# Layer 1's query, key and value projections by Strassen's scheme: seven products of quarters instead of eight

## The chip, the core and the metric

The kernel runs on one core of one Trainium2 chip. The metric is the device time of one execution in microseconds (us), where lower is better. The engines of a core are named as the profile names them: PE (TensorE, matmuls and transposes), PEld (TensorE's weight loads), DVE (VectorE), ACT (ScalarE), POOL (GpSimd) and SP (SyncE, which issues most DMAs).

## The reference, cut to what matters

The program has two layers over 2048 tokens of width 1024. Layer 0 has two attention mixers; the change only puts some extra preparation into it. Layer 1 is differential attention, and its input projection is what is changed:

```python
def odd_layer(x, norm_g, w_in, w_out, qn, kn, ...):
    h = rms_norm(x, norm_g)                       # 2048 x 1024
    proj = h @ w_in                               # w_in: 1024 x 4096
    q, k, v, gate = jnp.split(proj, [1024, 2048, 3072], axis=-1)
    q = rms_norm(q.reshape(b, s, 8, 2, 64), qn)   # per 64 columns
    k = rms_norm(k.reshape(b, s, 8, 2, 64), kn)
    q1, q2 = apply_rope(q[:, :, :, 0], cos, sin), apply_rope(q[:, :, :, 1], cos, sin)
    k1, k2 = apply_rope(k[:, :, :, 0], cos, sin), apply_rope(k[:, :, :, 1], cos, sin)
    ...                                           # attention, gate, w_out, residual
```

Everything is float32. The kernel keeps float32 accuracy with three matmuls for each one: a number is split into a high part H (rounded to the matmul's type, fp32r) and a low part L (what is left), and a product is aH·bH + aH·bL + aL·bH.

## The kernel before, in words

Layer 0's projection runs first (0 to about 560 us), then layer 0's attention with its output projection (to about 1168 us), then layer 1's projection (1168 to 1733 us), then layer 1's attention, gate and output projection.

`_project` serves both layers. The tokens are four blocks of 512, taken in two halves of two blocks. For each half, `hidden` loads a block in four tiles of 128 tokens (line 320), normalizes it (ScalarE squares it, line 323, VectorE scales it, line 325), transposes it on TensorE (line 330) and splits the result into H on ScalarE (line 334) and L on VectorE (line 335). Then groups of 512 weight columns follow; in layer 1 these are values, queries, queries, keys, keys, values. `weights_by` loads a group's 1024 x 512 weights in four DMAs on SP's queue (line 301) and splits them (H on ScalarE, line 307, L on GpSimd, line 309). The L of line 309 reads two tiles in SBUF, as the operations of lines 375, 379 and 381 do. The weights of a group are loaded once per half.

`project_tile` makes one tile of 128 tokens x 512 columns in one bank of PSUM: for each of eight k-tiles, `mm3` issues three matmuls (lines 214 to 216) with 128 x 128 of the hidden tile as the stationary and 512 columns of weights as the moving operand. For queries and keys, `squares` (lines 358, 359) and `normed` follow on the tile: the scaling by the norm reads PSUM (line 369), the rotary part is two products on VectorE (line 375), one on GpSimd (line 379) and a sum (line 381), which in layer 1 alternates between GpSimd and VectorE. `pairs_out` transposes four finished tiles (line 388), splits them and stores them to scratch memory on SP's queue. Values are copied (line 507) and stored from ScalarE's queue.

Two further streams lie in `_project`: `later` splits weights for later stages and stores them, in layer 0 both output projections' weights and in layer 1 the gate's (`AHEAD` says before which groups); and hidden tiles are stored for the gate, which is computed beside layer 1's attention. The last half's first block stays in SBUF for it (`last_hidden`).

Engines execute in order. The framework orders the instructions of each engine by its own estimate of when they become ready, with the order of the source as priority; it can therefore place a transposition between two matmuls of another tile. Buffers come from pools with a fixed count (`bufs`); a pool's next tile waits until the oldest is free. Layer 1's pools lie where layer 0's lay, and the attention's where layer 1's projection lay, so the order in which pools are opened says what must be free before a load can start.

## Time and profile before

| | us |
|---|---|
| median of 3 runs | 2802.15 (2797.86 to 2806.56) |
| the profiled execution: its time | 2806.47 |
| the profiled execution: its span, first to last instruction | 2804.3 |
| TensorE busy in the span | 2691.3 |
| layer 1's projection: first to last matmul | 1168.7 to 1732.7 |

The span is what all views of the trace refer to. The mean granted clock of TensorE is 0.990 of full speed. A matmul's duration in the trace includes its way through the array and overlaps the next one, so a sum of durations isn't the time that TensorE takes; distances between starts are.

### The profile page before, as it was taken

Reading aid. Unit: us, or ns where it says so; the run is one execution under the profiler, and the core shown is the slowest. Engines: PE = TensorE matmul, PEld = TensorE weight load, DVE = VectorE, ACT = ScalarE, POOL = GpSimd, SP = SyncE. Lnnn points to the kernel's source line nnn. Section 1 sums busy time; section 2 is a strip of 40 time slices with the busy share of each in tenths; the row PEclk is TensorE's granted clock in tenths of the full one; section 3 lists DMA queues with packets and bytes.
Section 4 is the critical chain, followed back from the end, with each engine's and each line's share of the span. In section 5 each row is a group of like instructions: output and inputs, shape, how many; then the busy total and the mean of one; then the engine's idle time right before and its main releaser. Section 6 shows DMA issues by size and latency. Waiting matters only on the chain.

```text
span 2804.3 us, 43657 instructions
## 1 busy us (share of the span) xinstructions
PE 2691.3 (96%) x13384; PEld 2166.5 (77%) x13384; DVE 1822.1 (65%) x4520; ACT 1599.4 (57%) x3975; POOL 1431.7 (51%) x1519
## 2 busy tenths in 40 slices
PE   7999999999899999999999999999999999999998
PEld 6888887888788888788888888767676777676776
DVE  7752285336777776457834783478886887777762
ACT  5443544357767775333343332578886777776661
POOL 3641254245545454336453652367675666767671
PEclk9999999999999999999999999999999999999999
DMA  5673348739877774754495347788867676464542
GB/s 177 226 240 139 109 148 271 239 111 248 223 196 192 191 196 144 238 190 128 143 297 187 124 134 211 219 232 225 215 194 223 178 210 200 124 190 134 162 154 80
DMA packets 354041, 521.64 MB, mean 186 GB/s; under 512 B 42768, under 2 KB 137744, under 8 KB 353808
## 3 DMA queue, kind: packets, MB, share of 16 engines
q1 hardware_dynamic: 349200, 510.47, 60.6%
q10 hardware_dynamic: 4608, 8.39, 0.8%
q8 instruction: 107, 1.75, 0.3%
q14 instruction: 126, 1.03, 0.1%
HBM read 361.70 MB, written 157.02 MB: 185 GB/s over the span
## 4 chain that ended last, share of the span: by engine, by line
PE 69%; DMA 7%; DVE 3%; ACT 2%; issue 1%; POOL 1%; SPq 0%; ACTq 0%; DVEq 0%; POOLq 0%
PE cO L1005 8%; PE p1mm L216 6%; PE p1mm L215 6%; PE p1mm L214 6%; PE cS L949 4%; PE cS L950 4%; PE ctr L1001 4%; PE com L214 2%; PE com L215 2%; PE com L216 2%; PE mom L214 2%; PE mom L215 2%; PE mom L216 2%; PE mtrB L775 2%; PE cG L214 2%; PE cG L216 2%
## 5 line engine op out<-in xcount | busy, mean ns | idle before, releaser
L956 ACT ACTIVATE cP<-cS,cnm 128x512 f32<-128x512 f32 (+3 forms) x640 | 394.3, 621 | 145.2 <-DVE cnm L953 134.2
L953 DVE TENSOR_REDUCE cnm<-cS 128x1 f32<-128x512 f32 (+3 forms) x640 | 374.7, 602 | 61.5 <-PE cS L950 55.0
L989 POOL TENSOR_TENSOR cP<-cP,cP 128x512 f32<-128x512 f32 (+1 forms) x320 | 358.3, 1148 | 43.7 <-ACT cP L987 43.1
L988 POOL TENSOR_SCALAR cP<-cP,crl,cel 128x512 f32<-128x512 f32 (+3 forms) x288 | 209.9, 743 | 237.9 <-DVE crl L970 136.1
L214 PE MATMUL p1mm<-p1wH,p1hH 128*128 128x512 f32 x768 | 300.1, 392 | 1.2 <-ACT p1hH L334 1.2
L216 PE MATMUL p1mm<-p1wH,p1hL 128*128 128x512 f32 x768 | 300.4, 392 | 0.0
L215 PE MATMUL p1mm<-p1wL,p1hH 128*128 128x512 f32 x768 | 299.3, 390 | 0.0
L309 POOL TENSOR_TENSOR p0wL<-p0ws,p0wH 128x512 fp32r<-128x512 f32 (+1 forms) x140 | 169.9, 1241 | 247.5 <-ACT p0wH L307 228.4
L1005 PE MATMUL cO<-cpt,cv 128*128 128x512 f32 (+3 forms) x640 | 290.1, 538 | 2.9 <-DVE cpt L1003 2.8
L949 PE MATMUL cS<-ck,cqd 128*128 128x512 f32 (+3 forms) x640 | 265.2, 418 | 17.1 <-ACT cP L956 13.7
L1003 DVE COPY cpt<-ctr 128x512 f32<-128x512 f32 (+1 forms) x320 | 191.4, 605 | 112.5 <-PE ctr L1001 109.1
L214 PE MATMUL p0mm<-p0wH,p0hH 128*128 128x512 f32 (+1 forms) x640 | 237.8, 375 | 6.7 <-ACT p0vt L497 4.7
L216 PE MATMUL p0mm<-p0wH,p0hL 128*128 128x512 f32 (+1 forms) x640 | 238.8, 374 | 1.5 <-DVE p0hL L335 1.5
L950 PE MATMUL cS<-ck,cql 128*128 128x512 f32 (+3 forms) x640 | 233.7, 369 | 5.8 <-DMA cql<-qL 5.8
L215 PE MATMUL p0mm<-p0wL,p0hH 128*128 128x512 f32 (+1 forms) x640 | 238.8, 373 | 0.0
L1001 PEld LDWEIGHTS ctr<-ident,cP 128*128 128x128 f32 x1088 | 139.0, 142 | 120.4 <-issue 64.9
L309 POOL TENSOR_TENSOR p1wL<-p1ws,p1wH 128x512 fp32r<-128x512 f32 x112 | 154.4, 1402 | 137.8 <-ACT p1wH L307 126.6
L987 ACT ACTIVATE cP<-cP,cc 128x512 f32<-128x512 f32 (+1 forms) x320 | 189.1, 651 | 22.9 <-DVE cc L973 22.4
L1001 PE MATMUL ctr<-ident,cP 128*128 128x128 f32 x1088 | 177.1, 275 | 5.2 <-ACT csq L1034 3.6
L214 PEld LDWEIGHTS p1mm<-p1wH,p1hH 128*128 128x128 f32 x768 | 144.3, 188 | 29.9 <-ACT p1hH L334 1.4
L216 PEld LDWEIGHTS p1mm<-p1wH,p1hL 128*128 128x128 f32 x768 | 144.2, 188 | 29.4
L215 PEld LDWEIGHTS p1mm<-p1wL,p1hH 128*128 128x128 f32 x768 | 144.3, 188 | 29.1
(302 smaller groups left out, 6945.4 us busy)
## 6 DMA issues: line engine op xcount, KB each, us to landing
p1ws<-in_od_w_in_dram SPq DMA_DIRECT2D x56, 512.0 KB, 3.7
p0ws<-in_ev_w_in_dram SPq DMA_DIRECT2D x48, 512.0 KB, 4.6
ck<-kH SPq DMA_DIRECT2D x144, 128.0 KB, 3.6
ck<-kL SPq DMA_DIRECT2D x144, 128.0 KB, 3.8
cv<-v SPq DMA_DIRECT2D x72, 256.0 KB, 4.3
cqd<-qH SPq DMA_DIRECT2D x64, 256.0 KB, 5.9
cql<-qL SPq DMA_DIRECT2D x64, 256.0 KB, 7.8
cwH<-wgH SPq DMA_DIRECT2D x64, 256.0 KB, 5.4
```

The source lines that it names most:

```text
L214: mm(ps, aH, bH, start=first, stop=False)
L215: mm(ps, aH, bL, start=False, stop=False)
L216: mm(ps, aL, bH, start=False, stop=last)
L309: low.tensor_tensor(l[:, :width], ws[:, k, :width], f32(h[:, :width]), ALU.subtract)
L949: mm(ps, qd[:, m, js], kt[:, :wd], start=True, stop=False)
L950: self.anchor = mm(ps, ql[:, m, js], kt[:, :wd], start=False, stop=True).ins
L953: nc.vector.tensor_reduce(nm[:, m, z:z + 1], ps, AX.X, ALU.max, negate=True)
L956: exp = nc.scalar.activation(chunks[z][:, :wd], ps, AF.Exp, bias=nm[:, m, z:z + 1], accum_out=acc).ins
L988: nc.gpsimd.tensor_scalar(p1, p1, rl[:, 0:1], e1, ALU.mult, ALU.mult)
L989: nc.gpsimd.tensor_tensor(p1, p1, p2, ALU.add)
L1001: nc.tensor.transpose(turned[:, (j - j0) * P:(j - j0 + 1) * P], us[j][kt // 4][:, kk:kk + P], self.ident)
L1005: mm(O[:, j0 * P:], v, T[:, :wd], start=(kt == 0), stop=(kt == nkt - 1), skip_group_check=True)
```

## The change

`_project` is divided into `project0` (layer 0, as before, but for one new stream) and `project1` (layer 1, new).

**The scheme.** For two blocks of 512 tokens and a group of 512 weight columns, the hidden matrix A (512 tokens x 1024) and the weights B (1024 x 512) are cut into quarters: A's rows into 256 + 256 tokens, the inner dimension into 512 + 512, B's columns into 256 + 256. Instead of eight products of quarters there are seven, by Winograd's form of Strassen's scheme, with four sums of A's quarters (S1 to S4), four sums of B's (T1 to T4) and sums of the products. In `PRODUCTS`, each entry names A's quarter or sum, B's quarter (row, column) or the slot of B's sum, and the bank that accumulates it. Three banks per block (X, Y, Z) accumulate products; X is read several times in between.

**B's sums** are made in layer 0's projection: `weight_sums` has 24 steps, called before each block of a group (26 calls). **A's sums** are made by the new `hidden`, from the transposed quarters while they are in PSUM, and split into H and L (ScalarE and GpSimd). S2 lies in the place of quarter 21, which is only needed by the gate; it is stored and reloaded at the end.

**In each group** a product of a block is 24 matmuls: two token tiles, four k-tiles, three parts, with 256 columns of weights as the moving operand. Results are put together by ScalarE's copies from X and VectorE's additions to them. Norm and rotary part (`normed`) now work on whole quarters, 128 x 1024, and read SBUF.

**Besides:** each weight quarter or sum is loaded and split as one operand of 128 x 1024, one or two ahead; the gate's weights are split one operand at a time, before each query or key group, instead of in two lumps; PSUM is divided into 2 banks for transposes and 6 for products (before 4 and 4); rotary tables are made once per half; halves take blocks (3, 2) and (0, 1); in the attention, pools are opened in another order, and the gate's weights get a pool of their own, `gw`.

```diff
-    AHEAD = ((0, 2), (0, 3), (1, 2), (1, 3)), ((0, 5), (1, 0))
+    AHEAD = (0, 2), (0, 3), (1, 2), (1, 3)
...
+        self.s1["t"] = d("t1", [6, 4, 4, P, 256])
...
                 for bi, b in enumerate(blocks):
+                    if half or gi:
+                        next(sums, None)
...
+    def weight_sums(self, pool):
+        nc, W = self.nc, self.a["od_w_in"]
+        sub = lambda o, x, y, op=ALU.subtract: nc.gpsimd.tensor_tensor(o, x, y, op)
+        for g in range(6):
+            for k in range(4):
+                t = pool.tile([P, 2, 2, 256], F32, tag="ts", name="p0ts")
+                nc.sync.dma_start(
+                    t.rearrange("p r c d -> p r (c d)"),
+                    W[:, g * 512:(g + 1) * 512].rearrange("(r k p) c -> k p r c", r=2, p=P)[k],
+                )
+                b11, b12, b21, b22 = (t[:, r, c, :] for r in range(2) for c in range(2))
+                sub(b22, b22, b12)
+                sub(b12, b12, b11)
+                sub(b11, b22, b11, ALU.add)
+                sub(b21, b21, b11)
+                nc.sync.dma_start(self.s1["t"][g, :, k].rearrange("s p d -> p s d"), t.rearrange("p r c d -> p (r c) d"))
+                yield
+
+    PRODUCTS = (
+        ("11", (0, 0), None, "X"), ("12", (1, 0), None, "Y"), ("s2", None, 0, "X"), ("s3", None, 3, "X"),
+        ("22", None, 2, "X"), ("s1", None, 1, "Z"), ("s4", (1, 1), None, "Z"),
+    )
+    ORDERS = (0, 1, 2, 5, 3, 4, 6), (0, 1, 2, 3, 4, 5, 6)
...
+        st = pool("st", 3)
+        wp = pool("w", 8)
...
+        xp = pool("x", 6)
+        ptr = pool("ptr", 2, space=PSUM)
+        pmm = pool("pmm", 6, space=PSUM)
...
+        def operand(src, *to):
+            ws = st.tile([P, 4, Q], F32, tag="ws", name=n + "ws")
+            nc.sync.dma_start(ws, src)
+            H, L = (wp.tile([P, 4, Q], F32R, tag="w", name=n + "w" + part) for part in "HL")
+            nc.scalar.activation(H, ws, AF.Copy)
+            nc.gpsimd.tensor_tensor(L, ws, f32(H), ALU.subtract)
+            return H, L
...
+                dv = nc.vector.tensor_tensor
+                a21, a22 = turned(1, 0), turned(1, 1)
...
+                nc.scalar.activation(r21, a21, AF.Copy)
+                halves(a22, 4, hi)
+                dv(raws[1], a22, r21, ALU.add)
+                a11 = turned(0, 0)
+                halves(a11, 0, lo)
+                dv(raws[3], a11, r21, ALU.subtract)
+                dv(raws[2], raws[1], a11, ALU.subtract)
+                a12 = turned(0, 1)
+                halves(a12, 4, lo)
+                dv(raws[4], a12, raws[2], ALU.subtract)
...
+                for k in (2, 3, 1, 4):
+                    nc.scalar.activation(of(k, "H"), raws[k], AF.Copy)
+                    nc.gpsimd.tensor_tensor(of(k, "L"), raws[k], f32(of(k, "H")), ALU.subtract)
+                yield
...
+        def normed(C, r, tab):
+            v = C.rearrange("p t (h d) -> p (t h) d", d=HD)
+            sq = tq.tile([P, D], F32, tag="tq", name=n + "sq")
+            nc.scalar.activation(sq, C.rearrange("p t c -> p (t c)"), AF.Square)
+            ss = sm.tile([P, 16], F32, tag="qss", name=n + "qss")
+            nc.vector.tensor_reduce(ss, sq.rearrange("p (h d) -> p h d", d=HD), AX.X, ALU.add)
+            rs = self.rstd(sm, ss, 16, 1.0 / HD, n + "q")
+            nc.vector.tensor_tensor(v, v, rs.unsqueeze(2).to_broadcast([P, 16, HD]), ALU.mult)
...
+            for o in (0, 32):
+                nc.vector.tensor_tensor(
+                    t4[:, :, :, o:o + 32], c4[:, :, :, 32 - o:64 - o],
+                    St[:, 4 * r:4 * r + 4, o:o + 32].unsqueeze(2).to_broadcast([P, 4, 4, 32]), ALU.mult,
+                )
+            nc.gpsimd.tensor_tensor(
+                c4, c4, Ct[:, 4 * r:4 * r + 4, :].unsqueeze(2).to_broadcast([P, 4, 4, HD]), ALU.mult
+            )
+            flat = C.rearrange("p t c -> p (t c)")
+            nc.gpsimd.tensor_tensor(flat, flat, t2, ALU.add)
...
+                    opens = p in (0, 1, 5)
+                    if opens:
+                        ps[bank, bi] = pmm.tile([P, 2, Q], F32, tag="mm", name=n + "mm" + bank)
+                    acc = ps[bank, bi]
+                    for pr in range(2):
+                        for k in range(4):
+                            aH, aL = stationary(h[bi], name, k, pr)
+                            for i, (l, r_) in enumerate(((aH, wH), (aH, wL), (aL, wH))):
+                                mm(
+                                    acc[:, pr, :], l, r_[:, k, :], start=opens and pr == k == i == 0,
+                                    stop=k == 3 and i == 2, skip_group_check=True,
+                                )
+                    two = slice(2 * bi, 2 * bi + 2)
+                    kept = {0: "a", 2: "b", 3: "c", 4: "d"}.get(p)
+                    if kept:
+                        nc.scalar.activation(tile_(kept)[:, two, :], acc, AF.Copy)
+                    if p == 1:
+                        nc.vector.tensor_tensor(T["a"][:, two, :], acc, T["a"][:, two, :], ALU.add)
+                        whole("a", 0, 0, bi)
...
         ld = pool("ld", 2)
-        pp = pool("pp", 20)
+        kp = pool("kp", 4)
+        gw = pool("gw", 3)
+        sm = pool("sm", 8)
+        fin = pool("fin", 2)
         ot = pool("ot", 4)
         vp = pool("v", 4)
+        sb = pool("sb", 2)
+        pp = pool("pp", 20)
```

`whole` calls `normed` on a quarter (two blocks) once both blocks have it, and queues eight turns per query or key group: `turn` transposes four 128 x 128 pieces, splits and stores them, at most one after each product, from the third product on after the quarter was queued. The steps of a query or key group are (product, block) with both blocks of a product in a row; in a value group the second block follows two steps behind the first, which leaves its hidden tiles time.

More of the change, by code (lines that the diff above doesn't have):

```diff
@@ new lines, in tables @@
+            tabs["q"] = self.rope_tables(tb, self.gain["ev_a_q_norm"], -0.125, n + "tq")
+            tabs["k"] = self.rope_tables(tb, self.gain["ev_a_k_norm"], 1.0, n + "tk")
+        groups = [
+            ("qk", 0, 512, dict(tab="q", dH="aqH", dL="aqL", p0=0)),
+            ("akv", 512, 256, dict(tab="k", dH="akH", dL="akL", p0=0)),
+            ("qk", 1280, 512, dict(tab=None, gain=True, dH="bqH", dL="bqL", p0=0)),
+            ("qk", 1792, 512, dict(tab=None, dH="bkH", dL="bkL", p0=0)),
+            ("bv", 2304, 512, {}),
+            ("gate", 768, 512, dict(r0=0)),
+            ("gate", 2816, 512, dict(r0=512)),
+        ]
@@ L338, in hidden @@
                 pass
-            if layer == 1 and b:
-                tok = slice(b * BLK, (b + 1) * BLK)
-                nc.sync.dma_start(s["hH"][:, :, tok].rearrange("k p t -> p k t"), f32(hH))
-                nc.sync.dma_start(s["hL"][:, :, tok].rearrange("k p t -> p k t"), f32(hL))
             return hH, hL
@@ L443, in _project @@
                 h = [hidden(blocks[0], 0)]
-            if layer == 0 and not tabs:
+            if not tabs:
                 tables()
             h.append(hidden(blocks[1], 1))
-            self.last_hidden = h[0]
             for gi, (kind, c0, width, o) in enumerate(groups):
@@ L450, in _project @@
                 ready = None
-                if (half, gi) in self.AHEAD[layer]:
+                if (half, gi) in self.AHEAD:
                     next(ahead)
-                turns = list(enumerate(blocks))
-                if layer == 1 and half == 1 and gi == len(groups) - 1:
-                    turns.reverse()
-                for bi, b in turns:
+                for bi, b in enumerate(blocks):
+                    if half or gi:
+                        next(sums, None)
                     if kind == "gate":
@@ L513, in _project @@
-                if not tabs:
-                    tables()
-            turn()
+                        pairs_out(xs, 4 if kind == "qk" else 1, b, o)
+    def weight_sums(self, pool):
[15 more added lines that the diff above has]
+                yield
```

387 lines of the change are left out of this document (274 added, 113 removed).

## The prediction

> **What bounds the kernel now.** I read the page's busy times first, then the windows by stage, the waits of TensorE in layer 1's projection, that stage's own instructions, and last the timeline for the spacing of matmuls and for what VectorE and GpSimd do to each other.
>
> ```profile
> span 2804.3 us, 43657 instructions
> ...
> PE 2691.3 (96%) x13384; PEld 2166.5 (77%) x13384; DVE 1822.1 (65%) x4520; ACT 1599.4 (57%) x3975; POOL 1431.7 (51%) x1519
> ```
> ```profile
> core 0: us, PE busy (x) PEld busy (x) DVE busy (x) ACT busy (x) POOL busy (x), PEclk, DMA share, GB/s
> 0.00:640.00 640.00, 611.11 (x3063) 513.43 (x3064) 345.57 (x801) 299.21 (x693) 247.71 (x251) 0.99 0.56 185
> 1168.00:1735.00 567.00, 566.19 (x2685) 472.38 (x2686) 354.56 (x598) 199.12 (x408) 259.99 (x194) 1.00 0.55 179
> ```
> ```profile
> PE p1mm L214 <- ACT p1hH L334: 1.2, 1, 1.2
> ```
> The second window is layer 1's projection. TensorE is busy for 566.2 of 567 us at the full clock and waits once, for 1.2 us; GpSimd is busy for 260 us (46%). So this stage is TensorE's alone, and what is taken off TensorE there shortens the run, as long as no other engine takes its place. The stage's matmuls:
>
> ```profile
> L214 PE MATMUL p1mm<-p1wH,p1hH x768: 387/389/477, 1168.7 to 1732.3; 128*128 128x512 f32 x192
> ...
> L216 PE MATMUL p1mm<-p1wH,p1hL x768: 389/389/478, 1169.6 to 1732.7; 128*128 128x512 f32 x192
> ```
> Three lines of 768 make 2304 matmuls of 512 columns in 564 us. The duration in a row (389 ns) overlaps its neighbours; what counts is the distance from start to start:
>
> ```profile
> 1339.96 0.39 PE L214 MATMUL p1mm<-p1wH,p1hH 128*128 128x512 f32 x1
> ...
> 1344.49 0.39 PE L216 MATMUL p1mm<-p1wH,p1hL 128*128 128x512 f32 x1
> 1344.73 1.03 PE L388 MATMUL p1trq<-ident,p1xn 128*128 128x128 f32 x8
> 1345.52 0.48 PE L214 MATMUL p1mm<-p1wH,p1hH 128*128 128x512 f32 x1
> 1345.83 0.40 PE L215 MATMUL p1mm<-p1wL,p1hH 128*128 128x512 f32 x1
> ```
> From 1339.96 to 1344.49 are 20 distances: 0.2265 us each, so 2304 take 521.9 us. Eight transposes push the next matmul 1.03 - 0.23 = 0.80 us back and make its successor 0.08 late: 0.89 per eight. The stage has 368 (256 of queries and keys, 112 of hidden tiles): 40.8 us. Together 562.7 of the 564 measured, so spacing and transposes explain the stage.
>
> **The matmuls.** Each group of 512 columns and each half (two blocks) now runs 7 products x 2 blocks x 2 token tiles x 4 k x 3 parts = 336 matmuls, against 192 before, but of 256 columns. Over 6 groups and 2 halves: 4032. Before shows that size in layer 0's narrow key and value group, with the same operands:
>
> ```profile
> 83.74 0.28 PE L215 MATMUL p0mm<-p0wL,p0hH 128*128 128x256 f32 x1
> ...
> 88.54 0.28 PE L216 MATMUL p0mm<-p0wH,p0hL 128*128 128x256 f32 x1
> ```
> ```profile
> 84.83 0.19 PEld L216 LDWEIGHTS p0mm<-p0wH,p0hL 128*128 128x128 f32 x1
> 84.94 0.19 PEld L214 LDWEIGHTS p0mm<-p0wH,p0hH 128*128 128x128 f32 x1
> ```
> 40 distances in 4.80 us: 0.120 us. A weight load (0.19 us) starts every 0.12 as well, so it stays covered at this width. Halving the width costs 0.120 x 2 against 0.2265, 6% more per column, and eats half of the eighth that the scheme saves: 4032 x 0.120 = 483.8, **-38.1 us** (not the 65 that 7/8 of 521.9 would give). The Trainium skill (TensorE: Matmul & The Clock Gate, Back-to-back issue gap) gives N/2.4 + 2.5 ns for a full clock: 109 and 216 ns. By it the saving would be an estimated 57 us and the time some 19 us lower; the rows here are 11 ns above it at both widths, and the measurement decides.
>
> **Transposes.** The number is the same. They now come from two banks of PSUM instead of four, so they may run in fours, each with its own late successor: 46 more times 0.085 = 4 at most, 0 at least. I take +2.
>
> **Query and key groups: GpSimd and VectorE.** This is where the change adds most. Each weight operand is now loaded and split per half (84 operands of 1024 columns, and 8 for the gate, against 112 of 512), and GpSimd does both multiply and add of every rotary quarter.
>
> ```profile
> L309 POOL TENSOR_TENSOR p0wL<-p0ws,p0wH 128x512 fp32r<-128x512 f32 x124 | 157.7, 1300 | 235.6 <-ACT p0wH L307 216.4 <-DMA wo1L<-p0wL 9.9 <-ACT p0sq L358 9.0
> L309 POOL TENSOR_TENSOR p1wL<-p1ws,p1wH 128x512 fp32r<-128x512 f32 x112 | 154.4, 1402 | 137.8 <-ACT p1wH L307 126.6 <-DMA wgH<-p1wH 7.8 <-DMA kH<-p1eH 2.6
> ...
> L309 POOL TENSOR_TENSOR p0wL<-p0ws,p0wH 128x256 fp32r<-128x256 f32 x16 | 12.4, 788 | 12.0 <-ACT p0wH L307 12.0
> ```
> From 256 to 512 columns an operation grows by 512 ns, so 1024 take 1300 + 1024 = 2.32 us; twice the stage's mean, 2.80, is the upper end. A query or key group of a half has 8 operands and 4 quarters of two operations: 16 x 2.32 = 37.1 us. VectorE adds to that, since the two shut each other out:
>
> ```profile
> L381 DVE TENSOR_TENSOR p1xn<-p1xn,p1t x32: 1751/1762/1771, 1237.5 to 1695.5; 128x512 f32<-128x512 f32 x32
> ```
> ```profile
> L369 DVE TENSOR_TENSOR p1xn<-p1mm,p1q8r x64: 680/686/693, 1232.4 to 1691.0; 128x512 f32<-128x512 f32 x64
> ```
> ```profile
> L375 DVE TENSOR_TENSOR p1t<-p1xn,p1tqS x64: 412/419/1522, 1233.6 to 1600.6; 128x256 f32<-128x256 f32 x64
> ```
> ```profile
> L325 DVE SCALAR_TENSOR_TENSOR p1xt<-p1xt,p1xr,p1g_in x16: 1280/1285/2408, 1133.5 to 1482.2; 128x1024 f32<-128x1024 f32 x16
> ```
> ```profile
> 1237.47 1.28 POOL L381 TENSOR_TENSOR p1xn<-p1xn,p1t 128x512 f32<-128x512 f32 x1
> ```
> ```profile
> 1237.54 1.76 DVE L381 TENSOR_TENSOR p1xn<-p1xn,p1t 128x512 f32<-128x512 f32 x1 [0.81 <-POOL p1xn L379]
> ```
> With one input in PSUM (L369) a 512 wide operation takes 686 ns, never more. With both in SBUF (L381) it takes 1762, and the pair in the timeline shows why: GpSimd ends at 1238.75, VectorE at 1239.30, 0.55 later; it stood still until GpSimd was done. The Trainium skill (GPSIMD Engine Reference, Key points) says the same: the two share SBUF interfaces, with contention from VectorE instructions that have two SBUF inputs. The two rows speak against this change, because the scaling by the norm, until now from PSUM, will read a tile in SBUF. Per quarter VectorE needs 1.285 (1024 wide, L325) and two 512 wide at about 0.70 (between L375's 0.42 and L325): 2.68, four times 10.7, less 0.13 of each of the 12 that runs under GpSimd's end: 9.1. The shared way is thus taken for 46.2 us, against TensorE's 336 x 0.120 + 32 x 0.111 = 43.9. The group took until now:
>
> ```profile
> 1250.66 0.87 PE p1trq L388 x8
> ...
> 1392.01 0.87 PE p1trq L388 x8
> ```
> Three groups in 141.35: 47.1 us. TensorE's part sinks by 3.2, but the shared way lets it sink by 0.9 only. The transposes of a finished quarter wait for GpSimd's addition, and behind them on TensorE's queue stand the next products. If nothing absorbed it, 2.3 us in each of 8 groups is 18; the value groups, where GpSimd has 7 x 2.32 = 16 us of work beside 40 of TensorE, and the operands fetched ahead absorb some. Bounds 0 and, with 2.80 per operand and 2.6 per rotary operation, (43.2 + 10.7 - 43.9) x 8 = 80. Taken, nearest to 46.2 with half absorbed: **+9**.
>
> **Hidden tiles at the start and between the halves.** The sums of the hidden quarters are made here.
>
> ```profile
> L334 ACT ACTIVATE p1hH<-p1trh 128x512 fp32r<-128x512 f32 x29 | 16.0, 594 | 12.4 <-PE p1trh L330 10.0 <-DMA wgL<-p1wL 2.3
> ...
> L323 ACT ACTIVATE p1junk<-p1xt 128x1024 f32<-128x1024 f32 x13 | 13.8, 1058 | 13.8 <-DMA p1xt<-x 13.8
> ```
> A block cost ScalarE 4 x (1.06 + 2 x 0.59) = 9 us; now it is twice 2 x 1.06 + 9 x 0.6 = 15. Between the last use of the first block's old tiles and the first need of the second block's new ones lie 8 steps of 24 matmuls, 23 us, against 30 for the two blocks, of which the 8 of squares can run ahead. It just fits on paper; but the loaded rows, the raw sums and the products' results share six buffers, so each half block's load waits for the one before. Two places, 0 to 8 each: **+6**. Bank X is copied (0.59) between products 3 and 4, with only one step between them, in value groups at times none: +1 (0 to 5).
>
> **Layer 0.** 24 steps each load 512 KB, do four 256 wide operations on GpSimd (4 x 0.79 = 3.2 us) and store 512 KB.
>
> ```profile
> POOL p0wL L309 <- ACT p0wH L307: 200.7, 33, 35.1
> ...
> ACT p0wH L307 <- DMA p0ws<-in_ev_w_in_dram: 43.0, 20, 7.6
> ```
> ```profile
> SPq L301 <- POOL p0wL L309: 105.1, 44, 6.7
> ```
> GpSimd waits there for 200 us with nothing to do, which covers 24 x 3.2 = 76. SyncE's queue is the risk: each store waits for GpSimd, and behind it stand the weight loads (L301), for which ScalarE waits already. 0 if that stays covered, 24 x 3.2 = 76 if each step came bare; nearly all is covered: **+3**. Moved besides: the gate's weights leave two places for one eighth per query or key group (counted above); tables are loaded twice, off the path. The hand-over to the attention has a hole of its own:
>
> ```profile
> 1750.00:1760.00 10.00, 3.64 (x10) 2.36 (x10) 3.50 (x8) 4.77 (x12) 1.69 (x3) 0.62 0.51 155
> ```
> 6.4 us idle; the second block's tiles now come free only two steps before the end, and the first key and query loads go into their place. Between -6 and +6; 0 taken, as the gate's matmuls can fill it.
>
> **Sum:** -38.1 + 2 + 9 + 6 + 1 + 3 = -17. The profiled run took 2806.47 (span 2804.3), 4.3 above the median of 2802.15, so 2789; against the median 0.6% faster. What a measurement here can tell from no change is about 0.3%, 8.4 us: 2793.7 to 2810.6 counts as the same.
>
> **Rivals.** First, *the shared way sets the pace* (slower). Every GpSimd operation at the stage's contended duration, and a queue in order that idles while VectorE is shut out: a group of 50 us costs (50 - 43.9) x 8 = 49, so -38 + 49 + 12 = +23: 2829, from 2811 up to 2860 at 53.9. It decides from a group period of 47.2 on, where -38 + 12 is used up; I stand at 45, close by. For it: 46.2 of bare work, 1762 against 686. Against it: GpSimd is at 46% now, and over the whole stage its work (92 + 64 operations of 2.32 and 40 of 1.29) is 414 us, with VectorE's share some 500 of 527. Second, *given back at the seams*: hidden tiles 16, layer 0 8, bank 4, the rest as above, -38 + 2 + 9 + 28 = +1, or less: 2800 to 2808, no change. Six buffers for three uses speak for it, TensorE's one wait of 1.2 us at these places now against it. Third, *everything absorbed*: -38 + 2 + 3: 2773; the average over the stage speaks for it, four query and key groups in a row against.
>
> **Chances.** Forecast (2778 to 2796) 0.46, absorbed 0.16, seams 0.15, shared way 0.23. Faster: 0.16 and 0.42 of the 0.46; same: 0.04, the seams' 0.12 and 0.02 of the shared way; slower: the rest. The range goes from 2768 (absorbed, with a gain at the hand-over) to 2826, the nearer half of the first rival.
>
> **What would show it.** 4032 matmuls of 256 columns at 0.120 us; a query or key group's period of about 45 (at 50 the first rival holds); GpSimd near 85% busy in the stage, and VectorE's 1024 wide scaling well over 1.285 on average; TensorE's waits in the stage some 15 to 20 us, most of them transposes for GpSimd's addition. It would be wrong if 256 wide matmuls ran further apart, or if TensorE waited for weights that GpSimd still splits.

## The result and the profile after

The changed kernel takes 2922.34 us (median of 4 runs, 2917.79 to 2927.30), the kernel before in the same runs 2800.01: a ratio of 1.044 (95% interval 1.041 to 1.047). It is slower by 122 us, where 2789 was forecast. The profiled execution has a span of 2916.0 us, 111.7 more than before.

That execution was the fastest of the four. The page's first lines and its row of granted clock, then two windows: layer 0's first part and layer 1's projection (columns as in the prediction).

```profile
span 2916.0 us, 47395 instructions
...
PE 2696.0 (92%) x15112; PEld 2248.2 (77%) x15112; DVE 1933.4 (66%) x4436; ACT 1680.0 (58%) x4011; POOL 1651.3 (57%) x1603
...
PEclk9999999999999999799998999999999999999999
```
```profile
0.00:640.00 640.00, 600.72 (x2993) 502.57 (x2994) 359.13 (x768) 291.19 (x667) 317.62 (x336) 0.99 0.67 220
1177.00:1836.00 659.00, 560.05 (x4380) 549.59 (x4380) 441.26 (x513) 280.92 (x454) 418.64 (x191) 0.91 0.57 180
```

The projection went from 564 us to 663 (1176.9 to 1839.8), with TensorE idle for 99 of the 659 in the row and at 0.91 of its clock; before it was idle for less than one, at 1.00. In layer 0's window TensorE is busy for 600.7 us, against 611.1 before. What it waits for in layer 1's projection (each row: total us, how often, the longest):

```profile
PE p1trq L656 <- DVE p1eL L659: 45.0, 7, 10.1
PE p1trh L562 <- DVE p1xt L556: 38.6, 6, 11.6
...
PE p1mmX L759 <- ACT p1hH L567: 6.1, 8, 1.0
PE p1trq L656 <- POOL p1cd L649: 3.6, 5, 1.0
PE p1mmX L759 <- ACT p1cc L766: 2.5, 1, 2.5
PE p1trq L656 <- POOL p1cb L649: 1.4, 1, 1.4
```

Two waits carry it: the transposes of finished quarters (`p1trq`), whose two banks come free only when VectorE has made the low parts, and the transposes of x (`p1trh`), which wait for VectorE's scaling. The spacing of the matmuls is as forecast; from the timeline:

```profile
1199.77 0.28 PE L759 MATMUL p1mmX<-p1wH,p1hH 128*128 128x256 f32 x1
...
1202.17 0.28 PE L759 MATMUL p1mmX<-p1wH,p1hL 128*128 128x256 f32 x1
1214.09 2.89 PE L562 MATMUL p1trh<-ident,p1xt 128*128 128x128 f32 x12 [11.64 <-DVE p1xt L556]
...
1218.05 0.41 PE L759 MATMUL p1mmX<-p1wL,p1hH 128*128 128x256 f32 x1
...
1221.67 0.41 PE L759 MATMUL p1mmZ<-p1wL,p1s1H 128*128 128x256 f32 x1
```

20 distances in 2.40 us are 0.120. Behind the wait of 11.64 us the same matmuls run 0.213 apart (17 distances in 3.62 us), and the granted clock is half of full speed until they are back at 0.120:

```profile
1214.09:1222.10 8.01, 7.32 (x33) 6.69 (x34) 3.08 (x5) 5.24 (x9) 4.35 (x4) 0.50 0.59 193
```

The stage has 13 waits of 2.5 us and more; in the 4 us behind them the granted clock was 0.50 to 0.74. So each of these waits is paid a second time in clock.

VectorE's operations in the stage, and the one group of GpSimd that grew most:

```profile
L208 DVE TENSOR_TENSOR p1qu<-p1qu,p1qms 128x16 f32<-128x16 f32 x32 | 50.4, 1575 | 1.1
...
L633 DVE TENSOR_REDUCE p1qss<-p1sq 128x16 f32<-128x1024 f32 x32 | 38.8, 1213 | 13.3 <-ACT p1sq L631 13.3
L206 DVE TENSOR_SCALAR p1qms<-p1qss 128x16 f32<-128x16 f32 x32 | 30.5, 953 | 0.8
L207 DVE SCALAR_TENSOR_TENSOR p1qu<-p1qy 128x16 f32<-128x16 f32 x32 | 26.8, 836 | 1.8 <-ACT p1qy L205 1.7
L635 DVE TENSOR_TENSOR p1cb<-p1cb,p1qr 128x1024 f32<-128x1024 f32 x8 | 21.6, 2706 | 0.2
L209 DVE SCALAR_TENSOR_TENSOR p1qr<-p1qu,p1qy 128x16 f32<-128x16 f32 x32 | 18.5, 579 | 1.1
```
```profile
L517 POOL TENSOR_TENSOR p1wL<-p1ws,p1wH 128x1024 fp32r<-128x1024 f32 x92 | 227.4, 2476 | 104.2 <-ACT p1wH L516 94.6
```

An operation on 128 x 16 elements should be nothing; L208 takes 1.58 us on average. The timeline shows why (VectorE, then GpSimd):

```profile
1347.18 0.17 DVE L209 SCALAR_TENSOR_TENSOR p1qr<-p1qu,p1qy 128x16 f32<-128x16 f32 x1
...
1355.19 1.84 DVE L207 SCALAR_TENSOR_TENSOR p1qu<-p1qy 128x16 f32<-128x16 f32 x1
1357.07 2.34 DVE L208 TENSOR_TENSOR p1qu<-p1qu,p1qms 128x16 f32<-128x16 f32 x1
1359.44 0.18 DVE L209 SCALAR_TENSOR_TENSOR p1qr<-p1qu,p1qy 128x16 f32<-128x16 f32 x1
```
```profile
1354.60 2.40 POOL L649 TENSOR_TENSOR p1cc<-p1cc,p1t 128x1024 f32<-128x1024 f32 x1
1356.96 2.42 POOL L517 TENSOR_TENSOR p1wL<-p1ws,p1wH 128x1024 fp32r<-128x1024 f32 x1
```

L207 ends at 1357.03 with GpSimd's L649 (1357.00), L208 at 1359.41 with L517 (1359.38). With GpSimd idle they take 0.17, as L209 at 1347.18. The four tiny operations thus cost 126 us in place of some 22.

As a measure of the query and key groups I use three whole groups of a half (the second query group and both key groups), from the first copy out of bank X of the second query group to that of the last value group. TensorE alone needs 3 x 43.9 = 131.7 for them by the prediction's rows.

### The profile page after: what moved, and what is told of

It is laid out like the page before. It is cut to its first block, busy times and chain, and to the rows that moved or that the text cites. A ratio compares the mean times of both kernels' runs of the same rounds, so it can differ in the third digit from the quotient of the medians.

```text
span 2916.0 us, 47395 instructions
## 1 busy us (share of the span) xinstructions
PE 2696.0 (92%) x15112; PEld 2248.2 (77%) x15112; DVE 1933.4 (66%) x4436; ACT 1680.0 (58%) x4011; POOL 1651.3 (57%) x1603
## 5 line engine op out<-in xcount | busy, mean ns | idle before, releaser
L517 POOL TENSOR_TENSOR p1wL<-p1ws,p1wH 128x1024 fp32r<-128x1024 f32 x92 | 227.4, 2476 | 104.2 <-ACT p1wH L516 94.6
L759 PE MATMUL p1mmX<-p1wH,p1hH 128*128 128x256 f32 x576 | 168.1, 292 | 8.6 <-ACT p1hH L567 6.1
L516 ACT ACTIVATE p1wH<-p1ws 128x1024 fp32r<-128x1024 f32 x92 | 96.4, 1056 | 125.8 <-PE p1mmX L759 48.7
L759 PE MATMUL p1mmX<-p1wH,p1hL 128*128 128x256 f32 x576 | 166.2, 289 | 0.0
L759 PE MATMUL p1mmX<-p1wL,p1hH 128*128 128x256 f32 x576 | 166.2, 289 | 0.0
L1240 PEld LDWEIGHTS cS<-ck,cqd 128*128 128x128 f32 x640 | 122.1, 191 | 46.3 <-ACT cP L1247 16.3
L215 PEld LDWEIGHTS p0mm<-p0wH,p0hH 128*128 128x128 f32 x640 | 121.3, 190 | 31.0 <-ACT p0vt L447 9.5
```

Source lines behind the costliest of these rows:

```text
L215: mm(ps, aH, bH, start=first, stop=False)
L517: nc.gpsimd.tensor_tensor(L, ws, f32(H), ALU.subtract)
L759: mm(acc[:, pr, :], l, r_[:, k, :], start=opens and pr == k == i == 0, stop=k == 3 and i == 2, skip_group_check=True,)
L1240: mm(ps, qd[:, m, js], kt[:, :wd], start=True, stop=False)
```

## The experiments

The theories are named in the expectations: P (VectorE stands still behind GpSimd's running operation), W (only the sum of the work counts), S (the making of the operands at the two seams, which are the start of layer 1's projection and the change from its first half to its second), later B (bursts: VectorE is behind only where several quarters finish close together). All rows below: median, ratio to the kernel before with its interval, three groups in half 1 / half 2, and TensorE's waits for the scaling of x, with those that the profile puts down to its root. All times are in us.

| run | us | ratio | three groups | x waits |
|---|---|---|---|---|
| the change | 2922 | 1.044 (1.041 to 1.047) | 159.9 / 155.8 | 38.6 |
| e1 half operations | 2906 | 1.036 (1.030 to 1.042) | 150.1 / 149.4 | 38.7 |
| e2 no refinement | 2910 | 1.037 (1.032 to 1.043) | 151.5 / 145.6 | 39.4 |
| e3 low parts on VectorE | 2902 | 1.035 (1.028 to 1.042) | 146.3 / 145.2 | 39.2 |
| e4 x buffers | 2949 | 1.051 (1.043 to 1.059) | 160.4 / 155.8 | 53.8 |
| e5 before + sums | 2814 | 1.003 (1.002 to 1.005) | | |
| e6 before + pools | 2809 | 1.002 (1.000 to 1.004) | | |
| e7 loads first | 2911 | 1.038 (1.036 to 1.040) | 160.0 / 156.0 | 19.4 |
| e8 transposes later | 2934 | 1.046 (1.044 to 1.049) | 160.3 / 155.9 | 39.8 |
| f1 no head norm | 2863 | 1.019 (1.015 to 1.024) | 131.3 / 131.3 | 40.2 |
| f2 no norms, loads first | 2828 | 1.008 (1.006 to 1.010) | 131.3 / 131.3 | 8.6 |
| f3 = e2 + e3 + e7 | 2881 | 1.026 (1.022 to 1.029) | 146.0 / 145.8 | 19.7 |
| f4 pipelined halves | 2899 | 1.034 (1.032 to 1.036) | 160.6 / 155.8 | 6.2 |
| f5 = f4 + e2 + e3 | 2873 | 1.024 (1.022 to 1.026) | 144.8 / 145.4 | 6.1 |
| f6 = f4 + f1 | 2836 | 1.011 (1.009 to 1.013) | 131.3 / 131.3 | 13.0 |
| f7 = f5 + e8 | 2873 | 1.024 (1.021 to 1.027) | 146.3 / 142.4 | 4.5 |
| f8 = f5, rotary on VectorE | 2848 | 1.016 (1.013 to 1.019) | 130.1 / 131.3 | 10.4 |
| f9 = f4 + f10 | 2860 | 1.020 (1.018 to 1.023) | 136.1 / 133.6 | 11.7 |
| f10 GpSimd's work on VectorE | 2880 | 1.028 (1.025 to 1.031) | 136.1 / 133.6 | 42.6 |

The ratios' intervals of e1 to e4 and of e8 overlap the change's. What is read from these five rests on their groups and waits; their medians alone prove nothing.

**e1: GpSimd's operations in halves.**

```diff
-            nc.gpsimd.tensor_tensor(L, ws, f32(H), ALU.subtract)
+            for c in (0, 2):
+                nc.gpsimd.tensor_tensor(L[:, c:c + 2, :], ws[:, c:c + 2, :], f32(H[:, c:c + 2, :]), ALU.subtract)
```
(and the rotary's multiply and add likewise)

> The change's kernel, with the three 1024-element GpSimd operations of layer 1's projection (the operand's low part, the rotary's multiply and its add) cut into two of 512 elements each: the same work, in pieces of half the length. Theory P (VectorE's small operations of the norm, and its operations with two operands in SBUF, stand still until the GpSimd operation that is running ends; in the changed kernel the four tiny ones of the norm take 126 us instead of some 22, and the wait delays the low parts that the transposes' banks wait for): the tiny ones' mean falls to about half, a query or key group from 55 us to 50 to 52, the kernel by 20 to 40 us, to 2880 to 2900. Theory W (only the sum of GpSimd's and VectorE's work counts, however it is cut): the same 2922, or up to 10 us more for the added starts. Theory S (the loss is in the value groups and the making of the operands): the same time, groups at 55 us whatever the tiny ones do.

The four tiny operations went from 3.94 us a quarter (1575 + 953 + 836 + 579 ns) to 3.32, not to half. The longest single one fell from 2.39 to 1.35 us, with the length of GpSimd's pieces, but the second piece follows the first at once and more of them meet one: L209's mean rose from 579 to 986 ns. Still the wait for the low parts fell from 45.0 to 16.0 us (the line of the waits below) and a group by 3 us, though GpSimd's work grew. That is P's sign, against W; but the kernel's 16 us is less than P said.

```profile
PE p1trq L659 <- DVE p1eL L662: 16.0, 12, 5.0
```

**e2: the root without refinement.**

```diff
-            rs = self.rstd(sm, ss, 16, 1.0 / HD, n + "q")
+            ln, rs = (sm.tile([P, 16], F32, tag="q" + t, name=n + "q" + t) for t in ("ln", "r"))
+            nc.scalar.activation(ln, ss, AF.Ln, bias=self.eps, scale=1.0 / HD)
+            nc.scalar.activation(rs, ln, AF.Exp, scale=-0.5)
```

> The change's kernel, with the head norm's reciprocal root taken from ScalarE's Ln and Exp alone: the refinement by four tiny VectorE operations (128x16) is left out, so the roots are a little less exact. Theory P: these four are 126 us of VectorE's time in the stage, nearly all of it standing still behind GpSimd; without them the query and key groups go from 55 us to 49 to 51 and the kernel falls by 30 to 50 us, to 2870 to 2890; part of the standstill moves to the next operation with two operands in SBUF, the norm's multiply. Theory W: the four are worth their free time only, 32 groups of four at 0.17 us, 22 us spread over 8 groups, so a group falls by at most 2.7 us and the kernel by 0 to 20 us. Theory S: the same 2922.

The groups fell from 52.6 to 49.5 us, as P said, the kernel by 12 only, where P had 30 to 50 and W 0 to 20; so this run doesn't part the two. The standstill moved on to the next operations with two inputs in SBUF: the rotary products on b with the key table (L643 there) went from 1.08 to 2.68 us on average.

**e3: the low parts on VectorE.**

```diff
-            nc.gpsimd.tensor_tensor(L, ws, f32(H), ALU.subtract)
+            nc.vector.tensor_tensor(L, ws, f32(H), ALU.subtract)
```

> The change's kernel, with the weights' low parts in layer 1's projection (84 subtractions of 1024 elements, and 8 for the gate weights) on VectorE in place of GpSimd. It takes 227 us off GpSimd and puts 92 operations of about 1.2 us, some 110 us, on VectorE, which works 540 to 550 of the stage's 659 us now, standstills included. Theory P: far fewer standstills, since GpSimd then works about 190 us of the stage; query and key groups 46 to 48 us, the kernel 50 to 75 us faster, 2850 to 2870. Theory W (the sum of the two engines' work is what limits a group): the sum falls from about 46 to 40 us a group, so the groups go to 44 to 47 us and the kernel falls by about as much; what tells it from P is the run with the halved operations. Theory S: the groups may fall but the value groups stay at some 58 us each and the waits of the operands' transposes at 38 us, so that at least 40 us of the loss stays. If VectorE is the limit by its own count, nothing falls: 2910 to 2940.

L208 fell from 1575 to 241 ns:

```profile
L208 DVE TENSOR_TENSOR p1qu<-p1qu,p1qms 128x16 f32<-128x16 f32 x32 | 7.7, 241 | 0.9
```
Groups of 48.6 us and -20 us: the direction of P, but short of 46 to 48, and P and W aren't parted. The waits for x stayed, as S said.

**e4: eight buffers for x, six for the weights.**

```diff
-        wp = pool("w", 8)
+        wp = pool("w", 6)
...
-        xp = pool("x", 6)
+        xp = pool("x", 8)
```

> The change's kernel, with eight buffers in place of six in the pool that the inputs' tiles, the raw sums and the results' quarters share, and six in place of eight for the weights' operands. Theory S (the operands are made late at the two seams since the loads of x wait for one of six shared buffers): the waits of the transposes of x for their scaling fall from 38.6 us to 15 to 25 and the kernel by 15 to 30 us, to 2890 to 2907. Theory P: the query and key groups stay at 55 us and the kernel within 10 us of 2922; fewer weight operands can cost up to 10 us. A variant of S in which the chain load, square, scaling, transposes is what is long, and not the buffer: the waits stay at 30 to 40 us.

The median is 26 us higher, and the waits for x rose to 53.8. The two sizes changed together and moved the pools behind them, so this says nothing on the shared buffers by itself.

**e5 and e6: the kernel before, with the sums alone and with the pools alone.** e5 adds `weight_sums`, its scratch tensor and its pool to the kernel before; e6 opens the attention's pools as the changed kernel does:

```diff
+        kp = pool("kp", 4)
+        gw = pool("gw", 3)
+        sm = pool("sm", 8)
+        fin = pool("fin", 2)
...
-        place = {(h, NB - 1): (ld, ("wH", "wL")) if h < 3 else (kp, ("k0", "k1")) for h in (0, 1, 2, 6, 7)}
+        place = {(h, NB - 1): (gw, ("wH", "wL")) if h < 3 else (kp, ("k0", "k1")) for h in (0, 1, 2, 6, 7)}
```

> The kernel before, with the weights' sums made in layer 0 as in the changed kernel (96 GpSimd operations, their loads and stores, two buffers more) and used by nobody: layer 1's projection stays as it was. It prices layer 0's part alone. In the two traces layer 1's projection starts 8.2 us later in the changed kernel (1176.9 against 1168.7 us). If the sums are what costs that: 8 us, 2805 to 2812 us. If it is the first operands of layer 1, which wait for something else: 0 to 4 us, 2800 to 2805.

> The kernel before, with only the changed kernel's new order of the attention's pools and its own pool for three gates' weights. It prices the hand-over's part alone: from the end of the projection to the end the changed kernel takes 1076 to 1080 us, the kernel before 1069 to 1072. If the new order is the cause: 6 to 11 us more than before, 2806 to 2812. If the cause is that the first queries and keys leave the projection late: the same within 4 us.

The sums cost 9 us (5 to 13), the pools 5 (0 to 11); the medians are 2 us above and inside the expected ranges.

**e7: a block's four loads first.**

```diff
+            loaded = {}
+            for p in range(2):
+                for e in range(2):
+                    t = b * NTB + 2 * e + p
+                    loaded[p, e] = xp.tile([P, D], F32, tag="x", name=n + "xt")
+                    nc.sync.dma_start(loaded[p, e], x[t * P:(t + 1) * P, :])
```

> The changed kernel, with the four loads of x for one block's operands issued ahead of that block's two halves in place of two and two. Theory S1 (a half's operands are late since its loads are only issued when the half before is nearly done, and take 5 to 6 us to land): the chain of a half, 16 us long, gets some 6 us shorter for every second half; waits of the transposes of x 38.6 to 20 us, kernel 15 to 30 us faster, 2890 to 2907. Theory S2 (the chain is ScalarE's squares, VectorE's root and scaling, and the transposes' own evictions, and a load that lands early only waits): the waits stay above 33 us and the time within 8 us. Four loads at once also take four of the six shared buffers, and the first sums get the last two: if these are short, 5 to 10 us slower.

The waits for the scaling fell by 19 us as S1 said (12.2, and 7.2 now put down to the root), and 4.7 of it came back as waits for the raw sums (5.1, before 0.4); the kernel gained 11, where S1 had 15 to 30.

**e8: transposes six products behind.**

```diff
-                                later.append((count[0] + 3, (T[up], T[low], bj, b, hp, o, o["p0"] + 2 * c + hp)))
+                                later.append((count[0] + 6, (T[up], T[low], bj, b, hp, o, o["p0"] + 2 * c + hp)))
```

> The changed kernel, with the transposes of finished quarters put six products behind them in place of three (one number). Theory B (bursts): a group's four quarters don't finish evenly; three of the four norms come within 14 us, each some 8 us of VectorE's queue with its standstills, so VectorE is some 10 us behind when the first transposes need their low parts, although over a whole group its work fits. Then three products more, 8.6 us, let VectorE catch up: the wait of the transposes for the low parts falls from 45 us to under 15, query and key groups from 54 to 47 to 50 us, the kernel by 25 to 50 us, to 2870 to 2900. Theory W (VectorE and GpSimd are short over the whole group): the wait only moves to a later place (the quarters' buffers, the shared banks), groups stay at 52 to 54 us and the kernel within 8 us of 2922.

Nothing moved in the groups; the kernel's median is 12 us higher. Theory B fell here, and again in f7.

**f1 and f2: the norms left out.** f1 returns at the head of `normed`; f2 also drops the squares and the root of x, on top of e7's loads:

```diff
-                    nc.vector.scalar_tensor_tensor(xs[e], xs[e], r[:, e:e + 1], gain, ALU.mult, ALU.mult)
+                    nc.vector.scalar_tensor_tensor(xs[e], xs[e], 0.02, gain, ALU.mult, ALU.mult)
```

> The changed kernel with the norm and the rotary embedding of the queries and keys left out altogether: the quarters go to the transposes as the products leave them. It leaves out 10 VectorE, 3 ScalarE and 2 GpSimd operations for each of 32 quarters. Theory P and theory W both: the query and key groups are held by this work, so they fall from 54 us to TensorE's own 44 to 45 and the kernel by 75 to 85 us, to 2835 to 2850; the value groups and the waits for the scaling of x stay (38 us of waits). If the groups were held by the quarters' way through the shared banks, their buffers or the 256-wide products themselves, they would stay above 48 us and the kernel above 2865.

> The kernel of the run without the head norm, in which also the norm of x is left out (its squares and its reciprocal root; a constant stands in their place, the scaling stays) and a block's four loads of x are issued first. If the seams are the serial way load, squares, root, scaling, transposes: the waits of x's transposes fall from 38 us to 10 to 18, and the kernel by another 25 to 45 us against the run without the head norm, to 2795 to 2820. If the scaling and the transposes' evictions are what is slow: 0 to 15 us. With both left out, what remains over the forecast's 2773 for everything absorbed is layer 0's and the hand-over's part, some 20 us, and the seams' rest.

The three groups of f1, and its whole stage, in the windows' columns:

```profile
1318.49:1449.83 131.34, 131.34 (x1106) 131.34 (x1105) 29.04 (x42) 50.63 (x73) 57.52 (x25) 1.00 0.72 217
1185.11:1782.01 596.90, 548.35 (x4404) 541.00 (x4404) 159.48 (x257) 234.75 (x358) 260.81 (x127) 0.94 0.66 200
```

TensorE is busy for all 131.34 us: 43.8 a group. So the groups' loss is the head norm's, 59 us of time; I had put 75 to 85 on it. (It leaves out eight VectorE operations a quarter, not ten: 513 in the change's stage, 257 in f1's.) f1's stage still takes 596.9 us against 526.6 for TensorE alone (483.8 + 40.8 + 2 by the prediction), and waits 40.2 us for x; with the norm of x out and the loads early, another 36 us go. So S has its own share. f2 came out 8 us above its range.

**f3 to f6: do the edits add up, and is the seam a question of order?** Here a half is one of the two pairs of 128-token tiles from which a block's operands are made. On top of e7's loads, f4 issues such a half's squares, root and scaling ahead of the transposes of the half before it, and begins one product earlier at the change of the projection's halves:

```diff
+            ready_ = {0: scaled(0)}
+            yield
+            for p in range(2):
+                if p == 0:
+                    ready_[1] = scaled(1)
+                xs = ready_[p]
```

> The changed kernel with three of the edits tried before together: the weights' low parts on VectorE, the head norm's root from ScalarE alone (the refinement left out), the loads of x first. One by one they gave 20, 12 and 11 us. Theory P (VectorE's standstills behind GpSimd): the first edit already took most of the standstill, so the second gives only its remaining 64 us of VectorE's time, and together the groups come to 47 to 48 us, the kernel to 2870 to 2885. Theory W (VectorE's queue as a whole): each edit adds its part in full, 43 us, to 2879 or less. In no case does it come under the kernel before: the seams still cost some 50 us, layer 0 and the hand-over some 15 to 20.

> The changed kernel with the making of the operands pipelined by one half: loads of x first, and the squares, the root and the scaling of a half issued before the transposes of the half ahead of it, the first ones one product earlier at the mid seam. All work is kept. Theory S1 (issue order: each half's chain only starts when the half before has been transposed, so 16 us a half lie bare): the waits for the scaling fall from 38 us to 5 to 15 and the kernel by 25 to 45 us, to 2877 to 2897; of that the early loads alone gave 11. Theory S2 (what a half costs is its transposes, four sums and eight evictions on ScalarE and VectorE, 12 us whatever comes first): within 8 us of the run with the loads first, 2903 to 2919.

> The run before this one with also the weights' low parts on VectorE and the head norm's root from ScalarE alone (the refinement left out). If the causes add: f4's time less 30 to 35 us (these two edits with the loads first gave 2881 where the loads alone gave 2911), 2845 to 2870. If they share the same cover: less than 20 us below f4. In no case under the kernel before by the sums so far: 2803 plus layer 0 9, pools 5, and what is left of the head norm, about 30.

> The pipelined making of the operands with the head norm and the rotary left out: the seams alone. Without the pipelining that was 2863, and with the norm of x left out and the loads first 2828. Theory S1: 2825 to 2840. Theory S2: 2848 to 2863. TensorE alone would give 2773 and with layer 0's and the pools' 14 us 2787; what stays above it is the seams' own way, transposes, sums, evictions and the slow clock behind each wait.

f4's wait for the scaling:

```profile
PE p1trh L575 <- DVE p1xt L561: 6.2, 2, 4.0
```
It fell from 38.6 us, with all work kept, and the kernel by 23; without the head norm the same edit gives 27 (2863 to 2836). So the waits for the scaling were a question of when the work is issued (S1), the kernel's gain just short of its range; the seams as a whole were that only in part, since f6's stage still takes 569.2 us against 526.6. In the groups the edits did not add: e3 alone gave 48.6, e2 and e3 together 48.6 again. f3's kernel nevertheless gained 41 of the 43 us that W's sum asks for, inside P's range too, and f5 came out 26 us under f4, between its two theories; neither run parts P and W. In f5's timeline the standstill has moved to what stands next beside GpSimd's rotary, the norm's multiply:

```profile
1302.98 3.43 DVE L650 TENSOR_TENSOR p1cb<-p1cb,p1qr 128x1024 f32<-128x1024 f32 x1
...
1314.95 1.21 DVE L650 TENSOR_TENSOR p1ca<-p1ca,p1qr 128x1024 f32<-128x1024 f32 x1
```

**f7 and f8: what holds the groups at 48.5.** f7 has e8's edit. f8:

```diff
-            nc.gpsimd.tensor_tensor(
+            nc.vector.tensor_tensor(
                 c4, c4, Ct[:, 4 * r:4 * r + 4, :].unsqueeze(2).to_broadcast([P, 4, 4, HD]), ALU.mult
             )
             flat = C.rearrange("p t c -> p (t c)")
-            nc.gpsimd.tensor_tensor(flat, flat, t2, ALU.add)
+            nc.vector.tensor_tensor(flat, flat, t2, ALU.add)
```

> The run with all the edits (2873 us), with the transposes of finished quarters put six products behind them in place of three. Theory B (bursts: VectorE is full for some 30 us of a group and then idle for some 10): with the standstills mostly gone the room of 8.6 us more is enough, the waits for the low parts fall from 23 us to under 10, three groups from 145 us to 135 to 140, the kernel by 12 to 28 us, to 2845 to 2861. Theory W (VectorE short over the whole group, 82% to 85% busy and the rest in places where it cannot be used): within 6 us of 2873; up to 10 us slower if the quarters' six buffers come free too late.

> The run with all the edits, with the rotary's multiply and add on VectorE too, so that GpSimd does nothing in the query and key groups. Theory P (the standstills are what is left: in that run the norm's multiply still takes up to 3.4 us in place of 1.2 and the low parts 2.8 in place of 1.2, some 18 us of 145 over three groups): VectorE loses these 18 us and gets 24 operations of 1.2 us, 29 us: about the same busy time, 45 us a group, in one queue without waits for the other engine: three groups 138 to 146 us, the kernel within 12 us of 2873. Theory W: VectorE's work per group goes from 34 us without standstills to 44, as much as TensorE's own 43.8; three groups 150 to 165 us and the kernel 10 to 45 us slower.

f7 changed nothing. f8 gave the busier engine more work, and the three groups went to TensorE's own time, 130 and 131 us; W had 150 to 165, and even P had only 138 to 146.

**f9 and f10: the engine move with all the computation kept.** f10 is the change with e3's and f8's diff and nothing else; f9 has f4's order too.

> The run with the pipelined making of the operands (2899 us), with the weights' low parts and the rotary's multiply and add on VectorE in place of GpSimd; all the computation kept. Theory P (two engines that stand still for each other): VectorE now does the whole of the norm in one queue, 34 us a group without standstills plus 10 for the rotary and 3 for the refinement, 46 to 47; three groups 131 to 142 us, the kernel 2848 to 2865. Theory W: VectorE's 47 us a group is over TensorE's 43.8, three groups 142 to 150, 2865 to 2885.

> The changed kernel with only this one edit: the weights' low parts and the rotary's multiply and add on VectorE in place of GpSimd. Nothing is left out and the order of the operands' making is the changed kernel's. Theory P: three groups from 160 and 156 us to 131 to 142; the standstills gone, the kernel 40 to 58 us faster, 2864 to 2882; the waits for the scaling of x stay at 38 to 40 us. Theory W: VectorE has more work than before, three groups 142 to 155; 2885 to 2915. Nothing near 2803 in either case, since the value groups' waits stay.

The change, then f10: three groups of each half, and f10's tiny operations.

```profile
1304.79:1464.66 159.87, 137.86 (x1107) 137.05 (x1105) 141.13 (x146) 67.71 (x108) 117.23 (x49) 0.93 0.57 178
1639.59:1795.43 155.84, 137.54 (x1107) 136.25 (x1105) 135.78 (x139) 67.75 (x108) 116.34 (x49) 0.95 0.57 183
```
```profile
1315.44:1451.56 136.12, 135.38 (x1138) 135.14 (x1136) 124.80 (x187) 65.27 (x104) 0.00 (x0) 1.00 0.63 200
1622.58:1756.15 133.57, 132.85 (x1117) 132.61 (x1115) 122.24 (x180) 65.58 (x105) 0.00 (x0) 1.00 0.65 206
```
```profile
L208 DVE TENSOR_TENSOR p1qu<-p1qu,p1qms 128x16 f32<-128x16 f32 x32 | 5.5, 171 | 0.2
...
L206 DVE TENSOR_SCALAR p1qms<-p1qss 128x16 f32<-128x16 f32 x32 | 5.4, 170 | 0.1
```

GpSimd is idle in these windows, where it was busy for 117 us. VectorE has 41 operations more, and its own busy time fell from 141 to 125 us, since the standstills went. TensorE is busy for 135.38 of 136.12 us at a clock of 1.00: f10's windows are longer than f1's 131.34 since another order of instructions puts more of TensorE's work into them (1138 and 1117 instructions against 1106), not since it waits.

The wait for the low parts is at 6.0 us, and the kernel gained 42 us by this edit alone; the waits for x, forecast at 38 to 40, are 42.6, so S's part is untouched. f9 adds the two edits: 2860. No version comes under the kernel before.

The edit takes away two things at once, the standstills and GpSimd's slower pace. That the pace matters little is argued from waits: TensorE waited 5.0 us for GpSimd's additions in the change and 45.0 for VectorE's low parts, and the later transposes of e8 changed nothing; no run parts the two.

## Why the prediction was wrong, by its own steps

In spans, 111.7 us more: the stage starts 8.2 later, takes 98.5 longer (564.4 to 662.9) and leaves 5.0 more behind it (1071.2 to 1076.2). The stage, from its first to its last matmul:

```profile
1176.93:1839.81 662.88, 563.25 (x4404) 552.59 (x4404) 441.95 (x513) 280.92 (x454) 418.64 (x191) 0.92 0.57 180
```

- **Matmuls, -38.1, and transposes, +2: right.** 0.120 us apart; f1's group takes 43.8 against 43.9 worked out. TensorE's own need fell from 564.4 to 526.6.
- **Query and key groups, +9 (0 to 80): the step that failed first.** It set 46.2 us for the way that GpSimd and VectorE share, by three VectorE operations a quarter (2.68 us), and took 45 for a group. A group took 52.6, and the head norm cost 59 us of the kernel's time: 66 of the stage (662.9 against f1's 596.9, which f1's trace enters 8.2 later), 51 of them idle and 15 in slow matmuls. The four tiny operations of the root were not in the list: they have almost no work of their own, but shut out they took 3.94 us a quarter, more than the three counted. The trace before already showed them standing still, at 1.42 us together (two tiles) where four times 0.17 is 0.68:

```profile
L206 DVE SCALAR_TENSOR_TENSOR p1q8u<-p1q8y 128x16 f32<-128x16 f32 x32 | 16.9, 528 | 6.5 <-ACT p1q8y L204 6.3
L207 DVE TENSOR_TENSOR p1q8u<-p1q8u,p1q8ms 128x16 f32<-128x16 f32 x32 | 12.8, 399 | 0.8
L205 DVE TENSOR_SCALAR p1q8ms<-p1qss 128x16 f32<-128x16 f32 x32 | 9.3, 292 | 1.1
L208 DVE SCALAR_TENSOR_TENSOR p1q8r<-p1q8u,p1q8y 128x16 f32<-128x16 f32 x32 | 6.6, 206 | 0.8
```
  And the price doesn't fall on a sum: it falls on VectorE's queue, 47 us busy in a group (141.13 / 3). Behind it in order stand the low parts, behind these two banks, and behind the banks TensorE. The first rival named that ("a queue in order that idles while VectorE is shut out") and its 50 to 53.9 us a group hold for 52.6; its total of 2811 to 2860 does not, since the seams come on top. What I held against it, GpSimd's 414 us over the stage, was sized right (418.6) and proved nothing. f10 shows that the loss goes when GpSimd's part moves. Of the 17 us between its 42 and f1's 59, only 1.5 are idle time in the three groups of both halves; f10's stage is 612.7 us, with TensorE 7 us longer idle and 9 longer busy than in f1, and that was not taken apart further.
- **Hidden tiles at the seams, +6 (0 to 16): failed as badly.** It compared ScalarE's work with the time at hand, "It just fits on paper". What counts is a chain, one half behind the other: load, two squares, root, scaling, transposes, 18.0 and 16.3 us from one to the next, as the scalings at the changed kernel's second seam show:

```profile
1514.76 2.48 DVE L556 SCALAR_TENSOR_TENSOR p1xt<-p1xt,p1xr,p1g_in 128x1024 f32<-128x1024 f32 x2
...
1532.79 2.48 DVE L556 SCALAR_TENSOR_TENSOR p1xt<-p1xt,p1xr,p1g_in 128x1024 f32<-128x1024 f32 x2
...
1549.13 2.48 DVE L556 SCALAR_TENSOR_TENSOR p1xt<-p1xt,p1xr,p1g_in 128x1024 f32<-128x1024 f32 x2
```
  f1, without the head norm, lost 70 us in the stage (596.9 against 526.6), 49 idle (596.9 - 548.35) and 22 in slow matmuls (548.35 - 526.6); 40.2 of the idle time are waits for x. The earlier issue takes 23 to 27 us of it away (f4, f6). The rest, transposes, sums, evictions and the clock behind them, is not split further.
- **The clock** had no term. A long wait costs itself and the matmuls at 0.213 us behind it: over the stage 99.6 us idle and some 37 in slow matmuls (563.25 - 526.6).
- **Bank X, +1:** 2.5 us of waits in one place; right in size. **Layer 0, +3 (0 to 76):** 9 (5 to 13) by e5, inside its bounds but three times the 3 that were taken. The single traces spread more: the stage starts 8.2 us later in the change's, 13.5 to 21.4 in those of its variants, and 18.1 in e5's, where what follows the stage is 11.5 shorter. **Hand-over, 0 (-6 to +6):** the pools cost 5 (0 to 11); in e6's trace this lies ahead of the stage, so the 5.0 behind the change's stage stay open.

In sum -38 + 66 + 70 + 8 + 5 = +111, the head norm's 66 and the seams' 70 taken from f1's stage (662.9 - 596.9, 596.9 - 526.6).

The Trainium skill (SBUF — State Buffer, Who interferes with whom) states that VectorE and GpSimd take one pair of ports exclusively for a whole instruction, that a VectorE instruction with two SBUF inputs contends with a GpSimd one that reads SBUF, and one-input forms only in a two-port mode. The trace agrees for L208 (two inputs, 1575 ns against 171 in f10) and for L633's reduction, which didn't stand still (1213 ns in the change, 1214 in f10). L206 (one input, 953 ns against 170) stood still too; no row shows in which mode it ran.

## What to carry to other kernels

Where a trace shows two engines excluding each other, as VectorE and GpSimd here, count instructions, not work: small operations in a chain waited for the rest of a long one on the other engine, and all that stood behind them in the queue waited too. Moving GpSimd's part to the busier VectorE can be faster, as f10 was by 42 us, since an operation of 1024 elements takes 1.22 us there in place of 2.4 and nothing stands still. A stage in which TensorE is 100% busy can cover serial chains and late queues that a cheaper stage lays bare: before taking 7% off it, cost the chain at each seam by its length, not by the engines' shares.

## What was not expected of the hardware

- A 128 x 16 operation on VectorE took from 0.16 to 2.39 us in one stage; in the timeline above the long ones end with a GpSimd operation of 2.4 us. Cutting these in two cut the four operations' time by 16% (3.94 to 3.32 us a quarter), not by half.
- After a wait of 11.64 us, matmuls of 256 columns ran at 0.213 us, with a granted clock of 0.50, and were back at 0.120 only at 1222.1, 8 us after TensorE began again; transposes with gaps lie between. The Trainium skill (TensorE: Matmul & The Clock Gate, What's actually happening) gives half the clock for an idle array and about 3.4 us of sustained work to leave it: the granted clock of 0.50 agrees, the 8 us here are longer, with gaps in the work.
